# Attention: the norms' steps in a lasting PSUM tile, the values loaded last, and the causal mask of the maxima added by VectorE in the maximum's own instruction

## The chip, the cores and the metric

The kernel runs on one core of a Trainium2 chip. Its time is the device time of one execution, in microseconds (us). The engines of the core are called as in the profile: PE (TensorE's matmuls), PEld (its weight loads), DVE or VectorE, ACT or ScalarE, POOL or GpSimd, SP or SyncE, which here only issues DMAs. The kernel before was timed three times: 2924.38, 2925.44 and 2928.65 us, a median of 2925.44 us.

## The reference: what is computed

One decoder layer on 2048 tokens of width 1024. A norm and an input projection `z = h @ W_in` feed three mixers side by side: eight heads of attention with a forgetting gate, four heads of mLSTM, four of HGRN2. Their outputs are joined, projected back and added to `x`; a gated feed-forward layer with a short convolution follows. The change lies in the eight attention heads:

```python
qa = _rms(_heads(a_q, A_HEADS), a_q_g)
ka = _rms(_heads(a_k, A_HEADS), a_k_g)
ca = jnp.cumsum(jax.nn.log_sigmoid(a_f.astype(f32)), axis=1).transpose(0, 2, 1)
...
s = jnp.einsum('bhqd,bhkd->bhqk', qi, k) * scale
s = s + ci[..., None] - c[:, :, None, :]
s = jnp.where(kpos[None, :] <= qpos[:, None], s, -jnp.inf)
p = jax.nn.softmax(s, axis=-1)
return jnp.einsum('bhqk,bhkd->bhqd', p, v)
...
ya = _rms(_merge(oa), g_a.reshape(A_HEADS, HEAD_DIM)).reshape(bsz, t, A_DIM)
```

So each head has scores with a causal mask, a softmax, a product with the values, and then a norm over the 64 columns of each token of the head's output.

## The kernel before, in words

The program runs through four stages: the input projection with the mLSTM and HGRN2 mixers woven in, the attention, the output projection with the second norm (`phase_out`), and the feed-forward layer. Inputs and results of a stage go through DRAM tiles (`s_qh`, `s_ql`, `s_kh`, `s_kl` for queries and keys, each number split in a high and a low part, `s_v` for values, `s_y` for the mixers' output).

**The attention** is written out by hand in one order (`manual_schedule`): what an engine does is queued in the order in which the code issues it. The unit is a step: 128 keys against a block of 512 queries. A head has 4 blocks of queries with 4, 8, 12 and 16 steps, so 40 steps, and eight heads have 320. In a step of the loop (lines 1041 to 1063)

- `att_scores` makes the transposed scores of the step, keys on partitions, on PE (lines 912 to 917), `exp` and a rounded copy on ACT (919, 921), and leaves the low part `pl` of the result to a subtraction (925). In three steps of four POOL does this at once, in the fourth VectorE does it one step later;
- `att_maxima` goes on with the maxima, which run up to 22 steps ahead (`LEAD`; 12 are made before the first step): PE makes one block of plain scores `m`, 128 queries by up to 512 keys (872). Where the block touches the diagonal, a second matmul adds the triangle mask `mnat` through an identity (876). VectorE takes the maximum of each row (877). When the maxima of 512 queries are there, they are joined (883), turned by PE into a row (889) and written into the rows 64 to 67 of `QB` by VectorE (890), so that the scores' matmul subtracts them;
- `att_values` multiplies the values with the results of three steps earlier (`SKEW`), three matmuls (938 to 940), the last of which needs `pl`.

One block is 40, 128 or 16 such steps later turned into the output: when the last values of a block are in, ACT copies them out one step later (946), and two steps after that PE turns them (952) into the PSUM tile `x`, out of which VectorE copies (955). `Later` is the list of such work that is put off by a number of steps.

**The norm of a head** (`att_finish`) starts four steps after its last values: reciprocals of the sums (978), squares on ACT (981), their totals (984), then `scale` (987, 988), and four `link`s, one a step, which run the iteration for the reciprocal root (`rms_steps`, lines 120 to 132: three operations before the loop, and three rounds of three). All tiles of it lie in SBUF, 128 partitions by 16 elements. Then `times` (997, 998) multiplies the output, POOL the gain (1003), and SP stores to `s_y` (1008). `scale` comes 9 steps after the head's last values. The last head does this per block, with 4 elements instead of 16.

**PSUM** has eight banks, all in use here: three for `m`, two for the scores, two for the values' products and one for the tile `x`, which holds the turned maxima (4 by 128) and the turned outputs (128 by 260) by turns.

**The loads of a head** (`att_load`) are issued on SP's queue, in this order: `QB`, `KB` (what the maxima need, and half of the scores), the first four blocks of the values `V`, `QA`, `KA` (the scores' other half), and the rest of `V`. An issue waits on SP until the buffer is free and its source has been written, and what is queued behind it waits too. Heads 0 and 1 are loaded ahead of the first maxima, head h+1 at the third step of head h.

**Before the attention** `consts` brings the masks in through a scratch tile `craw`; `state` clears the state `cstate` of HGRN2.

Of the kernel before, what the change touches and what calls it, by code (L numbers as in the profile page):

```python
# [10 lines left out]
F32 = mybir.dt.float32  # L11
# [218 lines left out]
def z_stats(k, pz, xbufs):  # L230

    nc = k.nc
    ss = k.t(pz, [P, 8], tag="n8s", bufs=1)
# [598 lines left out]
def att_load(k, h, st):  # L832
# [13 lines left out]
    ld(KB[68:70], k.s_fc[h])  # L846
    v = k.s_v[:, h, :].rearrange("(jt p) c -> p jt c", p=P)
    ld(V[:, 0:4], v[:, 0:4])
    ld(QA[0:64], k.s_qh[r])
    ld(QA[64:128], k.s_ql[r])  # L850
    ld(KA[0:64], k.s_kl[r])
    ld(KA[64:128], k.s_kh[r])
    ld(V[:, 4:16], v[:, 4:16])


def att_maxima(k, sts, pa, ps, later):

    nc = k.nc
    for st in sts:
        for qb in range(4):  # L860
# [4 lines left out]
            for i in range(4):  # L865
                q0 = qb * BLK + i * P
                for kb in range(qb + 1):
# [4 lines left out]
                    nc.tensor.matmul(  # L872
                        m[:, 0:nn], QB[0:70, q0 : q0 + P], KB[0:70, kb * BLK : kb * BLK + nn], start=True, stop=not last
                    )
                    if last:
                        nc.tensor.matmul(m[:, n - P : n], k.identb, k.mnat, start=False, stop=True)
                    nc.vector.tensor_reduce(mx[:, i, kb : kb + 1], m[:, 0:n], axis=AX.X, op=ALU.max)  # L877
                    if i < 3 or not last:
# [51 lines left out]
def att_values(k, st, pa, ps, later, qb, j, c0, ph, pl):  # L930
# [27 lines left out]
    if h == AH - 1:  # L958
        att_finish(k, st, pa, 4 * qb, 4, later, 4)
    elif qb == 3:  # L960
        att_finish(k, st, pa, 0, 16, later, 4)


def att_finish(k, st, pa, t0, n, later, wait):

# [3 lines left out]
    bufs = 1 if n == 16 else 2  # L969
    pieces = [slice(i, i + 4) for i in range(0, n, 4)]  # L970

    def first():
        o = st["o"][:, t0 : t0 + n, :]
        w["num"] = o[:, :, 0:64]
# [3 lines left out]
        nc.vector.reciprocal(w["rl"], o[:, :, 64])  # L978

# [6 lines left out]
    def scale():  # L986
        nc.vector.tensor_tensor(w["ss"], w["ss"], w["rl"], op=ALU.mult)
        nc.vector.tensor_tensor(w["ss"], w["ss"], w["rl"], op=ALU.mult)
        w["s"] = k.t(pa, [P, n], tag=f"as{n}", bufs=bufs)
        w["chain"] = rms_steps(k, pa, w["s"], w["ss"], HD, 1.0, f"a{n}")  # L990

# [17 lines left out]

    i = wait  # L1010
# [17 lines left out]
def attention(k, pa, ps, side):  # L1028
# [528 lines left out]
def _trunk(ctx, tc, a, out):  # L1557
# [37 lines left out]
    with ExitStack() as ms:  # L1595
# [13 lines left out]
        with ExitStack() as zs:  # L1609
# [111 lines left out]
def state(k, mconst):  # L1721
# [14 lines left out]
    k.cstate = mconst("cstate", [P, 2, HD])  # L1736
    nc.vector.memset(k.cstate, 0.0)


def consts(k, a, cp, mconst, pz, psum, cm):  # L1740
# [3 lines left out]
    def cast(dst, src):  # L1744
        raw = cm.tile([P, P], F32, tag="craw", name=k.nm("craw"))[:, 0 : src.shape[1]]
# [4 lines left out]
    k.mnat = mconst("mnat", [P, P], BF16)  # L1750
# [99 lines left out]
```

## Time and profile before

| What | Number |
|---|---|
| the three timed runs, median | 2925.44 us |
| the profiled execution, its own time | 2926.52 us |
| its span in the trace | 2924.7 us |
| mean granted PE clock over the span | 0.979 |
| busy share of the span: PE, PEld, DVE, ACT, POOL | 96, 80, 68, 44, 49 % |
| the attention in the trace: first maximum's matmul, last values' matmul | 932.0 us, 1427.8 us |

The profile is of one execution, 1.8 us of which lie around the span and 1.1 us over the median. A row of a group gives the line, engine, operation and tiles, then the busy time, the mean of one, and the idle time of the engine ahead of them with what ended most of it. A row of a timeline gives the start, the duration, the engine, line and operation, and in brackets the idle time ahead of it and what ended it; PE's matmuls overlap, so the distance between two starts says more than a duration. A row of stretches gives the stretch, then its length and for each engine its busy time and number of instructions, then PE's granted clock (1.00 is full speed), the DMA engines' busy share and GB/s.

### The profile page before, as it was taken

Reading aid. Unit: us, or ns where it says so; the run is one execution under the profiler, and the core shown is the slowest. Engines: PE = TensorE matmul, PEld = TensorE weight load, DVE = VectorE, ACT = ScalarE, POOL = GpSimd, SP = SyncE. Lnnn points to the kernel's source line nnn. Section 1 sums busy time; section 2 is a strip of 40 time slices with the busy share of each in tenths; the row PEclk is TensorE's granted clock in tenths of the full one; section 3 lists DMA queues with packets and bytes.
Section 4 is the critical chain, followed back from the end, with each engine's and each line's share of the span. In section 5 each row is a group of like instructions: output and inputs, shape, how many; then the busy total and the mean of one; then the engine's idle time right before and its main releaser. Section 6 shows DMA issues by size and latency. Waiting matters only on the chain. (4 is left out here: it accounts for less than half of the span.)

```text
span 2924.7 us, 42911 instructions
## 1 busy us (share of the span) xinstructions
PE 2815.1 (96%) x15181; PEld 2344.7 (80%) x15181; DVE 1991.4 (68%) x3384; ACT 1280.3 (44%) x2167; POOL 1447.5 (49%) x1255
## 2 busy tenths in 40 slices
PE   8999998999999999999899899999999999999999
PEld 7899996989997666666688788888788788888887
DVE  7336787265777787778546676777787577777655
ACT  4223322131322878887423344444454343344443
POOL 2345462344354677776302466666475544444443
PEclk9999997999998999999999999999999999999999
DMA  5434444323225644451347444444778333333666
GB/s 161 126 96 144 136 127 133 102 95 116 89 89 154 119 97 89 87 109 27 108 166 233 146 161 159 160 150 157 258 249 270 110 103 108 108 105 120 233 211 210
DMA packets 346616, 411.08 MB, mean 141 GB/s; under 512 B 47650, under 2 KB 234096, under 8 KB 343232
## 3 DMA queue, kind: packets, MB, share of 16 engines
q1 hardware_dynamic: 292016, 318.45, 37.1%
q10 hardware_dynamic: 51952, 81.45, 7.6%
q0 software_dynamic: 2432, 8.42, 0.8%
q8 instruction: 120, 1.97, 0.3%
q14 instruction: 96, 0.79, 0.1%
HBM read 280.24 MB, written 127.98 MB: 140 GB/s over the span
## 5 line engine op out<-in xcount | busy, mean ns | idle before, releaser
L1248 POOL TENSOR_TENSOR w<-w,w 128x512 fp32r<-128x512 f32 x302 | 405.1, 1355 | 402.3 <-ACT w L1247 355.3
L1436 PE MATMUL ps<-w,w 128*128 128x512 f32 x1848 | 423.8, 391 | 3.6 <-ACT w L1427 1.9
L1436 PEld LDWEIGHTS ps<-w,w 128*128 128x128 f32 x1848 | 348.4, 189 | 78.2 <-ACT w L1427 2.4
L214 PE MATMUL w<-whi,hlo 128*128 128x256 f32 (+1 forms) x1280 | 374.3, 293 | 0.0
L214 PE MATMUL w<-whi,hhi 128*128 128x256 f32 (+1 forms) x1280 | 372.1, 291 | 2.0 <-DVE z L330 2.0
L214 PE MATMUL w<-wlo,hhi 128*128 128x256 f32 (+1 forms) x1280 | 372.7, 292 | 0.0
L925 POOL TENSOR_TENSOR pl<-pf,ph 128x512 fp32r<-128x512 f32 (+2 forms) x240 | 287.3, 1211 | 141.3 <-ACT ph L921 127.9
L1429 POOL TENSOR_TENSOR w<-w,w 128x512 fp32r<-128x512 f32 x154 | 215.6, 1407 | 204.5 <-ACT w L1427 165.8
L1247 ACT ACTIVATE w<-w 128x512 fp32r<-128x512 f32 x302 | 180.5, 627 | 263.5 <-POOL w L1248 86.0
L1428 DVE TENSOR_TENSOR w<-w,w 128x512 fp32r<-128x512 f32 x154 | 178.2, 1166 | 108.3 <-ACT w L1426 103.2
L214 PEld LDWEIGHTS w<-whi,hhi 128*128 128x128 f32 x1280 | 248.6, 194 | 3.7 <-DVE z L330 2.4
L214 PEld LDWEIGHTS w<-wlo,hhi 128*128 128x128 f32 x1280 | 248.5, 194 | 1.6 <-issue 0.2
L214 PEld LDWEIGHTS w<-whi,hlo 128*128 128x128 f32 x1280 | 248.4, 194 | 1.3 <-issue 0.2
L877 DVE TENSOR_REDUCE mx<-m 128x1 f32<-128x512 f32 (+2 forms) x320 | 190.7, 605 | 85.4 <-PE m L872 59.1
L195 POOL TENSOR_TENSOR wlo<-wraw,whi 128x512 fp32r<-128x512 f32 (+1 forms) x112 | 147.9, 1352 | 147.0 <-ACT whi L193 124.5
L1253 DVE TENSOR_TENSOR w<-w,w 128x512 f32<-128x512 f32 x176 | 151.5, 879 | 86.6 <-DMA w<-in_w_up_dram 76.8
L919 ACT ACTIVATE pf<-s 128x512 f32<-128x512 f32 (+1 forms) x320 | 172.4, 539 | 85.1 <-PE s L913 49.4
L921 ACT ACTIVATE ph<-pf 128x512 fp32r<-128x512 f32 (+1 forms) x320 | 185.1, 578 | 12.9 <-DMA s_v<-h 2.7
L1294 DVE SCALAR_TENSOR_TENSOR u<-ps,fcol,u 128x1023 f32<-128x1023 f32 x88 | 108.9, 1278 | 95.0 <-ACT u L1293 95.0
L940 PE MATMUL pv<-pl,V 128*65 128x512 f32 (+1 forms) x320 | 120.3, 376 | 25.9 <-DVE pl L925 25.1
L1427 ACT ACTIVATE w<-w 128x512 fp32r<-128x512 f32 x154 | 96.7, 628 | 110.9 <-PE ps L1436 88.5
L1426 ACT ACTIVATE w<-w 128x512 fp32r<-128x512 f32 x154 | 95.8, 622 | 93.0 <-POOL w L1429 45.6
(374 smaller groups left out, 7062.3 us busy)
## 6 DMA issues: line engine op xcount, KB each, us to landing
w<-in_w_up_dram SPq DMA_DIRECT2D x182, 256.0 KB
w<-s_g SPq DMA_DIRECT2D x154, 256.0 KB
w<-in_w_down_dram SPq DMA_DIRECT2D x110, 256.0 KB
wraw<-in_w_in_dram SPq DMA_DIRECT2D x48, 512.0 KB
s_g<-u ACTq DMA_DIRECT2D x88, 256.0 KB
w<-s_w SPq DMA_DIRECT2D x88, 256.0 KB
s_g<-w ACTq DMA_DIRECT2D x66, 256.0 KB
x<-in_x_dram SPq DMA_DIRECT2D x32, 512.0 KB
```

Source lines behind the costliest of these rows:

```text
L195: nc.gpsimd.tensor_tensor(lo[:, q + i : q + i + 2, :], raw[:, i : i + 2, :], h[:, i : i + 2, :].bitcast(F32), op=ALU.subtract)
L214: nc.tensor.matmul(out, lsl(lhs[a], i), rsl(rhs[b], i), start=(i == 0 and j == 0), stop=(i == n - 1 and j == 2))
L877: nc.vector.tensor_reduce(mx[:, i, kb : kb + 1], m[:, 0:n], axis=AX.X, op=ALU.max)
L919: nc.scalar.activation(pf[:, c0:], s[:, c0:], AF.Exp)
L921: nc.scalar.activation(ph[:, c0:], pf[:, c0:], AF.Copy)
L925: eng.tensor_tensor(pl[:, c0:], pf[:, c0:], ph[:, c0:].bitcast(F32), op=ALU.subtract)
L1247: nc.scalar.activation(h, t, AF.Copy)
L1248: nc.gpsimd.tensor_tensor(lo, t, h.bitcast(F32), op=ALU.subtract)
L1253: nc.vector.tensor_tensor(t, x, y, op=op)
L1428: nc.vector.tensor_tensor(gl, gr, gh.bitcast(F32), op=ALU.subtract)
L1429: nc.gpsimd.tensor_tensor(wl, wr, wh.bitcast(F32), op=ALU.subtract)
L1436: nc.tensor.matmul(tiles[tile], g[x][:, tile * P : (tile + 1) * P], w[y], start=j == 0 and c == 0, stop=j == nj - 1 and c == 2,)
```

## The change

Five edits in the attention, and what makes room for them.

1. `att_maxima`: the mask's matmul is gone. Where the block touches the diagonal, VectorE's maximum becomes one instruction that adds the mask (`mnat`, now 512 wide with zeros in front) to the block in PSUM, writes the sum back there, and gives the maximum. The built program has it as two rows, the instruction and one that writes its result out.
2. The turned maxima (`put`) take a buffer of `m`'s three instead of the tile `x`.
3. The bank of `x` is now one tile that lasts through the attention, `k.px`: 260 columns for the turned outputs, and three slices of 48 columns in which `scale` and the `link`s of a norm keep their sums and results (`rms_psum`). `scale` computes the reciprocals a second time, into PSUM. The very last block still works in SBUF.
4. `scale` of a whole head comes 15 steps after its last values instead of 9.
5. `att_load` issues both pieces of `V` last. Of head 0, the second piece is issued after the first twelve maxima; head 1 is loaded in the seventh step instead of ahead of everything.

Room in SBUF comes from `craw`, whose part `cstate` takes (it is cleared after the masks are in), and from joining some small tiles.

```diff
@@ att_load
     ld(KB[68:70], k.s_fc[h])
-    v = k.s_v[:, h, :].rearrange("(jt p) c -> p jt c", p=P)
-    ld(V[:, 0:4], v[:, 0:4])
     ld(QA[0:64], k.s_qh[r])
...
     ld(KA[64:128], k.s_kh[r])
+    yield
+    v = k.s_v[:, h, :].rearrange("(jt p) c -> p jt c", p=P)
+    ld(V[:, 0:4], v[:, 0:4])
+    yield
     ld(V[:, 4:16], v[:, 4:16])
@@ att_maxima
-                        m[:, 0:nn], QB[0:70, q0 : q0 + P], KB[0:70, kb * BLK : kb * BLK + nn], start=True, stop=not last
+                        m[:, 0:nn], QB[0:70, q0 : q0 + P], KB[0:70, kb * BLK : kb * BLK + nn], start=True, stop=True
                     )
                     if last:
-                        nc.tensor.matmul(m[:, n - P : n], k.identb, k.mnat, start=False, stop=True)
-                    nc.vector.tensor_reduce(mx[:, i, kb : kb + 1], m[:, 0:n], axis=AX.X, op=ALU.max)
+                        nc.vector.tensor_tensor_reduce(
+                            out=m[:, 0:n],
+                            in0=m[:, 0:n],
+                            in1=k.mnat[:, BLK - n :],
+                            scale=1.0,
+                            scalar=NEG,
+                            op0=ALU.add,
+                            op1=ALU.max,
+                            accum_out=mx[:, i, kb : kb + 1],
+                        )
+                    else:
+                        nc.vector.tensor_reduce(mx[:, i, kb : kb + 1], m[:, 0:n], axis=AX.X, op=ALU.max)
...
-                pm = k.t(ps["x"], [4, P], tag="x")
+                pm = k.t(ps["m"], [P, BLK], tag="m")[0:4, 0:P]
@@ turn
-        pt = k.t(ps["x"], [P, 4, 65], tag="x")
+        pt = k.px[:, 0:260].rearrange("p (a d) -> p a d", a=4)
@@ rms_psum, new; att_finish
+    for _ in range(3):
+        yield
+        nc.vector.tensor_tensor(u, out, h, op=ALU.mult)
+        nc.vector.tensor_tensor(u, u, out, op=ALU.mult)
+        nc.vector.scalar_tensor_tensor(out, u, 1.5, out, op0=ALU.add, op1=ALU.mult)
...
+        k.pn = (k.pn + 1) % 3
+        pn = k.px[:, 260 + 48 * k.pn : 308 + 48 * k.pn].rearrange("p (a n) -> p a n", a=3)
+        ps, ms, w["s"] = (pn[:, i, 0:n] for i in range(3))
+        nc.vector.reciprocal(ms, w["sum"])
+        nc.vector.tensor_tensor(ss, ss, ms, op=ALU.mult)
+        nc.vector.tensor_tensor(ps, ss, ms, op=ALU.mult)
+        w["chain"] = rms_psum(k, pa, w["s"], ps, ms, f"a{n}")
...
-    i += 1
+    i = 15 if n == 16 else i + 1
     later.put(i, scale)
@@ attention
-        att_load(k, 0, sts[0])
-        att_load(k, 1, sts[1])
+        first = att_load(k, 0, sts[0])
+        next(first)
+        next(first)
+
+        k.px, k.pn = k.t(ps["x"], [P, BLK], tag="x"), 0
...
-                        if h and qb == 0 and j == SKEW - 1 and h + 1 < AH:
-
-                            att_load(k, h + 1, sts[h + 1])
+                        if (qb, j) == ((0, SKEW - 1) if h else (1, 2)) and h + 1 < AH:
+
+                            for _ in att_load(k, h + 1, sts[h + 1]):
+                                pass
```

**How the instructions move, on SP**, where the attention begins. Each row is the load of one piece for head 0 and, in brackets, the semaphores it waits for; `PE`, `Activation` and `Pool` there mean that a buffer must come free. Before:

```order
L840 DMA KB_9751<-s_fc 2x2048 [waits DMAHW3_49]
L840 DMA V_9752<-s_v 128x4x130 [waits PE_49,DMAHW4_49,Activation_49,Pool_49]
L840 DMA QA_9748<-s_qh 64x2048 [waits DMAHW5_49]
L840 DMA QA_9748<-s_ql 64x2048 [waits DMAHW6_49]
L840 DMA KA_9749<-s_kl 64x2048 [waits DMAHW7_49]
L840 DMA KA_9749<-s_kh 64x2048 [waits DMAHW0_49]
L840 DMA V_9752<-s_v 128x12x130 [waits DMASW6_49,DMASW7_49,DMASW4_49,DMAHW1_49,DMASW2_49,DMASW0_49]
```

and of the change:

```order
L840 DMA KB_9738<-s_fc 2x2048 [waits DMAHW3_49]
L840 DMA QA_9735<-s_qh 64x2048 [waits DMAHW4_49]
L840 DMA QA_9735<-s_ql 64x2048 [waits DMAHW5_49]
L840 DMA KA_9736<-s_kl 64x2048 [waits DMAHW6_49]
L840 DMA KA_9736<-s_kh 64x2048 [waits DMAHW7_49]
L840 DMA V_9739<-s_v 128x4x130 [waits PE_49,DMAHW0_49,Activation_49,Pool_49]
L840 DMA V_9739<-s_v 128x12x130 [waits DMASW6_49,DMASW7_49,DMASW4_49,DMAHW1_49,DMASW2_49,DMASW0_49]
```

The four loads of `QA` and `KA` are no longer behind the piece of `V` that waits for PE, ACT and POOL.

**On VectorE**, where the norm of head 0 begins while head 1 is worked on (`ass` holds the totals, `rl` the reciprocals, `mx` the maxima, `ao` the turned outputs, `pl` the low parts). Before, from `scale` on:

```order
L987 TENSOR_TENSOR ass_1694_10701<-ass_1694_10701,rl_1692_10699 128x16 [waits DVE_49]
L988 TENSOR_TENSOR ass_1694_10701<-ass_1694_10701,rl_1692_10699 128x16 [waits DVE_49]
L120 TENSOR_SCALAR a16m_10806<-ass_1694_10701 128x16 [waits DVE_49]
L121 TENSOR_SCALAR a16h_10807<-ass_1694_10701 128x16
L122 TENSOR_SCALAR as_1725_10805<-a16m_10806 128x16 [waits DVE_49]
L877 TENSOR_REDUCE mx_10601<-m_10821 128x1 [waits PE_49]
```

and of the change, where `x_9750` is the lasting tile:

```order
L937 TENSOR_TENSOR pl_10809<-pf_10805,ph_10807 128x512 [waits Activation_49,Pool_49]
L878 ISA m_10844,mx_10558<-m_10844,mnat 128x512 [waits PE_49]
L878 ISA mx_10558 128x1
L895 TENSOR_REDUCE m_1744_10847<-mx_10558 128x4 [waits DVE_49]
L1030 RECIPROCAL x_9750<-ao_10012 128x16
L1031 TENSOR_TENSOR ass_1682_10656<-ass_1682_10656,x_9750 128x16 [waits DVE_49]
L1032 TENSOR_TENSOR x_9750<-ass_1682_10656,x_9750 128x16 [waits DVE_49]
L981 TENSOR_SCALAR x_9750<-x_9750 128x16 [waits DVE_49]
L982 TENSOR_SCALAR a16h_10855<-x_9750 128x16 [waits DVE_49]
L983 TENSOR_SCALAR x_9750<-x_9750 128x16 [waits DVE_49]
L967 COPY ao_10721<-x_9750 128x260 [waits DVE_49,PE_49]
```

`scale` has six operations instead of five and now stands right ahead of the copy of the second block's output of head 1, out of the same bank.

**On PE** at that same place, the end of the step in which the second block of head 1 is turned. Before:

```order
L872 MATMUL m_10914<-KB_9767,QB_9766 128x512 [waits DVE_49]
L876 LDWEIGHTS identb
L876 MATMUL m_10914<-mnat,identb 128x128
L938 MATMUL pv_10879<-ph_10855,V_9768 65x512
L939 MATMUL pv_10879<-ph_10855,V_9768 64x512
L940 MATMUL pv_10879<-pl_10857,V_9768 65x512 [waits Pool_49]
L952 MATMUL x_10925<-ident,oT_10885 128x65 [waits Activation_49]
```

and of the change:

```order
L874 MATMUL m_10844<-KB_9933,QB_9932 128x512 [waits DVE_49]
L950 MATMUL pv_10813<-ph_10792,V_9934 65x512
L951 MATMUL pv_10813<-ph_10792,V_9934 64x512
L952 MATMUL pv_10813<-pl_10794,V_9934 65x512 [waits Pool_49]
L964 MATMUL x_9750<-ident,oT_10817 128x65 [waits DVE_49,Activation_49]
```

The mask is gone, and the transposes wait for VectorE as well as for ACT: in the built program for the last operation of `scale`, L983. This wait stands at the second block of each of the heads 1 to 7, so seven times, and nowhere else among the turns.

More of the change, by code (lines that the diff above doesn't have):

```diff
@@ L232, in z_stats @@
     nc = k.nc
-    ss = k.t(pz, [P, 8], tag="n8s", bufs=1)
+    ss = k.t(pz, [P, 16], tag="ss")[:, 0:8]
     for b in range(2):
@@ L958, in att_values, with rms_psum, att_finish @@
     if h == AH - 1:
-        att_finish(k, st, pa, 4 * qb, 4, later, 4)
+        att_finish(k, st, pa, 4 * qb, 4, later)
     elif qb == 3:
-        att_finish(k, st, pa, 0, 16, later, 4)
-def att_finish(k, st, pa, t0, n, later, wait):
+        att_finish(k, st, pa, 0, 16, later)
+def rms_psum(k, pool, out, ss, ms, tag):
+    nc = k.nc
+    h = k.t(pool, list(ss.shape), tag=tag + "h")
+    u = k.t(pool, list(ss.shape), tag=tag + "u")
+    nc.vector.tensor_scalar(out=ms, in0=ss, scalar1=1.0 / HD, scalar2=EPS, op0=ALU.mult, op1=ALU.add)
+    nc.vector.tensor_scalar(out=h, in0=ss, scalar1=-0.5 / HD, scalar2=-0.5 * EPS, op0=ALU.mult, op1=ALU.add)
+    nc.vector.tensor_scalar(
+        out=out.bitcast(I32), in0=ms.bitcast(I32), scalar1=-0.5, scalar2=float(0x5F3759DF), op0=ALU.mult, op1=ALU.add
+    )
+    for _ in range(3):
[3 more added lines that the diff above has]
+        nc.vector.scalar_tensor_tensor(out, u, 1.5, out, op0=ALU.add, op1=ALU.mult)
+    yield
+def att_finish(k, st, pa, t0, n, later):
     nc = k.nc
@@ L970, in att_finish @@
     pieces = [slice(i, i + 4) for i in range(0, n, 4)]
+    end = st["h"] == AH - 1 and t0 == 12
     def first():
         o = st["o"][:, t0 : t0 + n, :]
-        w["num"] = o[:, :, 0:64]
+        w["num"], w["sum"] = o[:, :, 0:64], o[:, :, 64]
         w["rl"] = k.t(pa, [P, n], tag=f"rl{n}", bufs=bufs)
@@ L977, in first @@
         w["ss"] = k.t(pa, [P, n], tag=f"ass{n}", bufs=bufs)
-        nc.vector.reciprocal(w["rl"], o[:, :, 64])
+        nc.vector.reciprocal(w["rl"], w["sum"])
     def square(c):
@@ L986, in scale @@
     def scale():
[L987 to L990, printed above, removed]
+        ss, rl = w["ss"], w["rl"]
+        if end:
+            nc.vector.tensor_tensor(ss, ss, rl, op=ALU.mult)
+            nc.vector.tensor_tensor(ss, ss, rl, op=ALU.mult)
+            w["s"] = k.t(pa, [P, n], tag=f"as{n}", bufs=bufs)
+            w["chain"] = rms_steps(k, pa, w["s"], ss, HD, 1.0, f"a{n}")
+            return
+        k.pn = (k.pn + 1) % 3
[5 more added lines that the diff above has]
+        w["chain"] = rms_psum(k, pa, w["s"], ps, ms, f"a{n}")
     def link():
@@ L1008, in store @@
         nc.sync.dma_start(k.s_y[t0 * P : (t0 + n) * P, r].rearrange("(tt p) d -> p tt d", p=P), w["sq"])
-    i = wait
+    i = 4
     later.put(i, first)
@@ L1039, in attention @@
             later.step()
+        for _ in first:
+            pass
         lead, pend, t = LEAD0, [], 0
@@ L1618, in _trunk @@
             z = z_groups(k, 0, pz, wp, psw, xb)
-            pz.tile([P, 120], F32, tag="padz", name="padz", bufs=1)
+            pz.tile([P, 128], F32, tag="padz", name="padz", bufs=1)
             state(k, mconst)
@@ L1749, in consts @@
     k.identb = mconst("identb", [P, P], BF16)
-    k.mnat = mconst("mnat", [P, P], BF16)
+    k.mnat = mconst("mnat", [P, BLK], BF16)
+    nc.vector.memset(k.mnat[:, 0 : BLK - P], 0.0)
     k.mtr = mconst("mtr", [P, P], BF16)
@@ L1754, in consts @@
     nc.vector.tensor_copy(k.identb, k.ident)
-    cast(k.mnat, a["mnat"])
+    cast(k.mnat[:, BLK - P :], a["mnat"])
     cast(k.mtr, a["mtr"])
@@ L1759, in consts @@
         cast(k.cmask[:, i, :], a["cmask"][:, i * HD : (i + 1) * HD])
+    nc.vector.memset(k.cstate, 0.0)
     k.sel8 = mconst("sel8", [72, BH])
@@ L1793, in consts @@
     lg = k.col[:, 24:26]
-    lm, lr, lb = mconst("lm", [P, 2]), mconst("lr", [P, 2]), mconst("lb", [P, 2])
+    lbs = mconst("lbs", [P, 6, 2])
+    lm, lr, lb, k.lba, k.lbb, k.lbn = (lbs[:, i, :] for i in range(6))
     nc.vector.tensor_tensor(lm, lg, lg, op=ALU.subtract)
```

5 lines of the change are left out of this document (2 added, 3 removed).

## The prediction

> **What bounds the kernel now.** I read the profile from the top: busy shares, then the stretches of the attention, then what PE waits for there, then the timelines of PE and VectorE around one of those waits. The page's first part:
>
> ```profile
> PE 2815.1 (96%) x15181; PEld 2344.7 (80%) x15181; DVE 1991.4 (68%) x3384; ACT 1280.3 (44%) x2167; POOL 1447.5 (49%) x1255
> ```
>
> PE is busy for 96% of the span, so time is won only by taking matmuls away or by closing PE's gaps. The stretches (length; busy us and count of PE, PEld, DVE, ACT, POOL; PE's clock; DMA share; GB/s) show where gaps are: the attention's start, its middle, and around one stall in the middle.
>
> ```profile
> 932.00:960.00 28.00, 24.14 (x88) 15.27 (x87) 19.90 (x41) 10.71 (x22) 13.82 (x21) 0.63 0.91 229
> 960.00:1378.00 418.00, 400.81 (x2116) 274.81 (x2115) 327.18 (x623) 338.86 (x644) 295.56 (x253) 0.98 0.44 87
> 1024.00:1029.00 5.00, 5.00 (x27) 3.18 (x26) 4.86 (x10) 4.30 (x9) 3.43 (x3) 1.00 0.83 223
> 1029.00:1032.00 3.00, 0.66 (x4) 0.16 (x3) 3.00 (x5) 1.20 (x2) 2.86 (x3) 1.00 0.00 0
> 1032.00:1035.60 3.60, 3.60 (x12) 2.19 (x12) 3.23 (x8) 1.23 (x2) 2.87 (x4) 0.57 0.01 2
> ```
>
> In the middle PE idles 418.00 - 400.81 = 17.2 us. The last three rows are one event: VectorE full for 5 us, then PE nearly idle for 3 us while VectorE is still full, then 3.6 us at clock 0.57. The second half of the event costs 3.60 x (1 - 0.57) = 1.55 us. What PE waits for in the whole attention (total, times, longest), and the waits themselves (idle time ahead in brackets):
>
> ```profile
> PE pv L940 <- DVE pl L925: 25.1, 17, 3.0
> ```
>
> ```profile
> 1031.89 0.45 PE L940 MATMUL pv<-pl,V 128*65 128x512 f32 x1 [2.34 <-DVE pl L925]
> 1341.27 0.33 PE L940 MATMUL pv<-pl,V 128*65 128x256 f32 x1 [0.23 <-DVE pl L925]
> 1382.46 0.33 PE L940 MATMUL pv<-pl,V 128*65 128x256 f32 x1 [3.04 <-DVE pl L925]
> 1392.34 0.44 PE L940 MATMUL pv<-pl,V 128*65 128x512 f32 x1 [2.50 <-DVE pl L925]
> 1399.45 0.44 PE L940 MATMUL pv<-pl,V 128*65 128x512 f32 x1 [1.51 <-DVE pl L925]
> 1404.49 0.33 PE L940 MATMUL pv<-pl,V 128*65 128x256 f32 x1 [0.99 <-DVE pl L925]
> ```
>
> Of the 17 waits, seven are long ones, one in each of the heads 1 to 7 (first and last: 1031.89 and 1382.46); seven are short like that at 1341.27; the last three rows are the last head's. So the long ones hold 25.1 - 5.0 - 7 x 0.24 = 18.4 us, 2.6 each. Why VectorE is late there:
>
> ```profile
> 1020.17 0.17 DVE L987 TENSOR_TENSOR ass<-ass,rl 128x16 f32<-128x16 f32 x1
> 1020.96 0.69 DVE L877 TENSOR_REDUCE mx<-m 128x1 f32<-128x512 f32 x1
> 1021.77 0.18 DVE L131 TENSOR_TENSOR a16u<-a16u,a16h 128x16 f32<-128x16 f32 x1
> 1023.70 1.22 DVE L131 TENSOR_TENSOR a16u<-a16u,a16h 128x16 f32<-128x16 f32 x1
> 1024.96 1.22 DVE L132 SCALAR_TENSOR_TENSOR as<-a16u,as 128x16 f32<-128x16 f32 x1
> 1030.09 1.75 DVE L925 TENSOR_TENSOR pl<-pf,ph 128x512 fp32r<-128x512 f32 x1
> 1033.87 0.41 DVE L955 COPY ao<-x 128x260 f32<-128x260 f32 x1
> ```
>
> ```profile
> L877 DVE TENSOR_REDUCE mx<-m 128x1 f32<-128x512 f32 (+2 forms) x320 | 190.7, 605 | 85.4 <-PE m L872 59.1 <-PE m L876 23.2
> ```
>
> The same 128x16 operation of a `link` takes 0.18 us at 1021.77 and 1.22 at 1023.70. Both have all their operands in SBUF. The 320 maxima, which read PSUM, keep to a mean of 605 ns. So the links sometimes wait for SBUF, the queue behind them slips, and `pl` comes 2.3 to 3.0 us late.
>
> **The change part by part**, against the profiled execution's own 2926.52 us (1.1 over the median).
>
> *The masks leave PE.* 128 matmuls of this kind go:
>
> ```profile
> L876 PE MATMUL m<-mnat,identb 128*128 128x128 bf16 x128 | 31.0, 242 | 0.0
> ```
>
> ```profile
> 1021.95 0.23 PE L876 MATMUL m<-mnat,identb 128*128 128x128 bf16 x1
> 1021.99 0.31 PE L938 MATMUL pv<-ph,V 128*65 128x256 f32 x1
> 1022.14 0.28 PE L939 MATMUL pv<-ph,V 128*64 128x256 f32 x1
> 1022.25 0.28 PE L940 MATMUL pv<-pl,V 128*65 128x256 f32 x1
> ```
>
> Since matmuls overlap, the 242 ns are an upper end (31 us in all). From start to start a mask takes 0.04 us, the lower end (5 us), and the matmul behind it 0.15 instead of the 0.11 of the next one. I take 0.07: **-9 us**.
>
> *VectorE gets the masks.* No masked maximum is in this trace. The nearest rows are a plain maximum (0.69 at 512 columns, above), an operation of VectorE on two inputs that writes into PSUM, and one with all operands in SBUF:
>
> ```profile
> L1330 DVE TENSOR_TENSOR ps<-ps,tmp 128x512 f32<-128x512 f32 x44 | 30.5, 693 | 0.4
> L1428 DVE TENSOR_TENSOR w<-w,w 128x512 fp32r<-128x512 f32 x154 | 178.2, 1166 | 108.3 <-ACT w L1426 103.2 <-issue 3.5 <-DMA s_g<-u 1.4
> ```
>
> The price lies between no more than now and 1.17 - 0.69 = 0.48 more each; I take the 693 ns, since it is the row with PSUM, and for the read-out that follows up to 0.17, as a 128x16 operation has. That is 128 x 0.17 = 22 us of VectorE's time, and 62 + 22 = 84 at the upper end. VectorE has 418.00 - 327.18 = 91 us of slack in the middle, so this hides unless it stands ahead of something that PE awaits (the last rival). The maxima run up to 22 steps ahead; that is the cover.
>
> *The norm's steps in PSUM.* They take no SBUF result any more but for `h` and `u`. If they stay at the 0.17 to 0.18 us of the undisturbed rows, as PSUM's maxima keep theirs, the 2.1 us that two operations lost at 1023.70 and 1024.96 are not lost, and `scale` and the links, which ran at 1020 to 1027, come six steps later, behind the `pl` that was late. Then the seven long waits and the last head's three go: 18.4 + 5.0 = **-23.4 us**; I leave the seven short ones. With the long ones goes the half clock behind them: 7 x 1.55 = **-10.9 us**. (After the last head's 2.50, 1.51 and 0.99 I count no drop; one row shows it, below.) The lower bound is nothing gained: third rival.
>
> ```profile
> 1392.30:1396.00 3.70, 3.22 (x14) 1.90 (x15) 3.63 (x8) 1.18 (x3) 2.98 (x4) 1.00 0.14 38
> ```
>
> *A new wait.* The transposes of the second block in heads 1 to 7 now wait for the last operation of `scale`, which is issued in the same step. On PE all the next steps are queued behind them, ACT and POOL wait for those. The pace of a step, before:
>
> ```profile
> 1024.83 0.40 PE L912 MATMUL s<-QB,KB 70*128 70x512 f32 x1
> 1025.30 0.40 PE L872 MATMUL m<-KB,QB 70*128 70x512 f32 x1
> 1026.24 0.39 PE L912 MATMUL s<-QB,KB 70*128 70x512 f32 x1
> ```
>
> A step is 1.41 us, and its maxima's matmul is done 0.9 in. Then VectorE does, in this order, the masked maximum (0.7), its read-out (up to 0.2), the join (0.2) and six operations of `scale` (five took 1020.96 - 1020.17 = 0.79, so about 1.0). It ends 3.0 us in, or 3.6 if the `pl` ahead of the maximum holds it up for 0.6. The transposes are due at 1.41, so PE waits 1.6 to 2.2; I take 2.0: 7 x 2.0 = **+14 us**. Idle times of 2.34 were followed by half clock, 2.50 once was not and 1.51 was not, so I give four of seven the drop: 4 x 1.55 = **+6.2 us**. The links behind it stand in the steps 16 to 19, three short operations each, and have that much slack.
>
> [...] Without the wait the sum would be 20 us lower.
>
> *The turned maxima* take one of three buffers of `m` for the time from PE's transpose to VectorE's write; that is 32 times, hidden by the 22 steps of lead, and it costs a wait of at most one step each if VectorE is late. I count nothing.
>
> *The start.* SP's queue, PE and ACT there:
>
> ```profile
> 915.06 0.25 SPq L840 DMA_DIRECT2D KB<-s_fc  x1
> 929.22 0.39 SPq L840 DMA_DIRECT2D V<-s_v  x1
> 931.49 0.59 SPq L840 DMA_DIRECT2D KA<-s_kh  x1
> ```
>
> ```profile
> 942.35 0.79 PE L913 MATMUL s<-QA,KA 128*128 128x512 f32 x1 [1.33 <-DMA KA<-s_kh]
> ```
>
> ```profile
> 947.59 0.63 ACT L921 ACTIVATE ph<-pf 128x512 fp32r<-128x512 f32 x1 [2.69 <-DMA s_v<-h]
> ```
>
> `V` stood for 929.22 - 915.06 = 14 us at the queue's head, and `QA`, `KA` behind it. Now they go ahead of it, past a wait that is not theirs. PE's busy time in 932 to 960 is 24.1 of 28 at clock 0.63, so much of this is work. I take the two waits, 1.33 + 2.69: **-4 us**, between 0 and -7 (with part of the 28 x 0.37 = 10 us of clock). Eight masked maxima among the first twelve, with no lead yet, cost 8 x 0.17: **+1 us**. Head 1's loads, moved from the start to the seventh step, and the second piece of `V` have some ten steps (14 us) until they are needed, and the DMA share of 0.44 leaves room: nothing. If that cover is short, the first maxima of head 1 or the values of head 0 wait, once each.
>
> Sum: -9 - 23.4 - 10.9 + 14 + 6.2 - 4 + 1 = -26.1, so 2900.4 for a profiled execution, 2899.3 for a median that lies 1.1 lower; **2900 us**.
>
> **The rivals.** Without the new wait the sum stands at 2880.2.
>
> *The new wait is longer.* `pl` and the maximum both late, 3.3 us each time and a clock drop each time: 7 x (3.3 + 1.55) = 34, 2914. For: VectorE was full for 7.9 of the 8 us from 1024 to 1032, at that very place. Against: the links that filled it have moved away.
>
> *No clock drop at the new wait.* With 1 us each time 2887; with 2 us and no drop 2894. For: 1.51 and 2.50 without a drop. Against: 2.34 with one. [...]
>
> *The norm's steps gain nothing.* They stay slow with `h` and `u` in SBUF, the old waits stay and the new one is added: 2880.2 + 34.3 + 20.2 = 2935. Against: every PSUM row keeps its time.
>
> *Slower: VectorE takes the masks badly.* If a masked maximum with its read-out costs 0.5 or more over the plain one, three or four in a row ahead of `scale` leave VectorE as late at the turn as it is today, when the copy at 1033.87 comes 5.9 us behind the transposes:
>
> ```profile
> 1027.94 0.41 PE L952 MATMUL x<-ident,oT 65*128 65x65 f32 x4
> ```
>
> Then PE waits 5.9 there: 7 x (5.9 + 1.55) = 52, 2932. It decides for slower from (2926.5 - 2880.2) / 7 - 1.55 = 5.1 us of wait in each head. For: 1166 ns of the SBUF row. Against: 693 of the PSUM row.
>
> **How the numbers follow.** Forecast 0.52; longer wait 0.20; no drop 0.12; no gain from PSUM 0.07; masks slow 0.09. The range holds the first three: down to the 2887 with 7 us more from the masks or the start, 2880; up to the 2914 with the masks at 5 instead of 9 and no gain at the start, 2922. A measurement can tell about 0.2%, 5.9 us, from no change: faster means below 2919.6, slower above 2931.3. Faster: 0.84 of the three, less 0.04 for their upper edges, 0.80. Slower: the two rivals' 0.16 lie around 2932 to 2935 with both signs near, 0.10. The same: 0.10.
>
> **What would show it.** Right: in the waits of PE the one on `pl` falls from 25.1 to a few us, and a new one of the transposes on VectorE appears, seven times, 14 us; the stretch of half clock follows some of them; a masked maximum with its read-out takes 0.7 to 0.9 us at 512 columns; the norm's 128x16 rows take 0.17 to 0.2; the first score of `QA` waits for no `KA`. Wrong: the old waits stay, or the new one is over 3 us; masked rows above 1.1 us; a new wait of PE on `m`, because VectorE returns its buffers late; or a start that does not move.

## The result and the profile after

| | Median, us | Range, runs |
|---|---|---|
| before | 2927.05 | 2924.38 to 2928.74, 4 |
| the change | 2910.06 | 2908.00 to 2916.08, 4 |
| ratio | 0.9950 | 95% interval 0.9936 to 0.9963 |

The change saves 17 us of the 26 that were forecast; the time lies inside the range. A second set of runs gave 2910.96 against 2925.08, a ratio of 0.9960 (0.9947 to 0.9972). The profiled execution took 2909.49 us with a span of 2907.7.

What PE waits for in the attention of the changed kernel (total, times, longest):

```profile
PE x L964 <- DVE x L983: 13.9, 7, 3.4
PE m L874 <- DVE mx L878: 5.6, 2, 5.5
PE pv L952 <- DVE pl L937: 5.2, 10, 1.0
PE pv L952 <- POOL pl L937: 3.3, 5, 1.3
```

The old waits on `pl`, 25.1 us on VectorE and 0.7 on POOL before, have shrunk to 5.2 and 3.3. The first row is the new wait: seven times, 13.9 us, where the forecast had seven times 2.0. Five of the seven last 1.67 us, one 2.13, and the last one 3.42. The second row is one wait of 5.5 us at the start that the forecast did not have.

VectorE and PE at one of the seven turns, with the step's first matmul on PE at the top:

```profile
1019.80 0.39 PE L924 MATMUL s<-QB,KB 70*128 70x512 f32 x1
...
1023.04 0.44 PE L964 MATMUL x<-ident,oT 65*128 65x65 f32 x4 [1.67 <-DVE x L983]
```

```profile
1019.91 0.68 DVE L937 TENSOR_TENSOR pl<-pf,ph 128x512 fp32r<-128x512 f32 x1
1020.71 0.70 DVE L878 CUSTOM_DVE_ANT_0 m<-m,mnat 128x512 f32<-128x512 f32 x1
1021.32 0.14 DVE L878 DVE_READ_ACCUMULATOR2_ANT mx<- 128x1 f32 x1
1021.50 0.17 DVE L895 TENSOR_REDUCE m<-mx 128x4 f32<-128x16 f32 x1
1021.58 0.25 DVE L1030 RECIPROCAL x<-ao 128x16 f32<-128x16 f32 x1
...
1022.71 0.18 DVE L983 TENSOR_SCALAR x<-x 128x16 int32<-128x16 int32 x1
1023.51 0.43 DVE L967 COPY ao<-x 128x260 f32<-128x260 f32 x1 [0.62 <-PE x L964]
```

Masked maximum, read-out, join and the six operations of `scale` follow each other without a gap and end 3.1 us into the step. PE was ready for the transposes 1.67 us before they began, at 1021.37, so 1.57 us into the step (the forecast had 1.41). No operation of the rows shown is slow; PE waits because they stand in the same step and the built order has its transposes wait for the last of them. At the last of the seven turns (1370.43) a `pl` of 1.66 us stood ahead of them, and the wait is 3.42.

The groups on VectorE (count, then busy time and mean ns); the second row is the plain maximum:

```profile
L878 DVE CUSTOM_DVE_ANT_0 m<-m,mnat 128x512 f32<-128x512 f32 x32 | 22.2, 693 | 2.3 <-PE m L874 1.5
L889 DVE TENSOR_REDUCE mx<-m 128x1 f32<-128x512 f32 x192 | 130.7, 686 | 61.9 <-PE m L874 59.5
L878 DVE DVE_READ_ACCUMULATOR2_ANT mx<- 128x1 f32 x128 | 17.9, 140 | 0.0
L990 DVE SCALAR_TENSOR_TENSOR x<-a16u,x 128x16 f32<-128x16 f32 x21 | 3.7, 178 | 0.7
```

A masked maximum of 512 columns takes 693 ns, and its read-out 140 ns. The links' last operation has a mean of 178 ns, where it had 522 before:

```profile
L132 DVE SCALAR_TENSOR_TENSOR as<-a16u,as 128x16 f32<-128x16 f32 x21 | 11.0, 522 | 0.7
```

The clock behind four of the seven waits, two with and two without a drop (length, then for each engine busy time and count, then the clock, DMA share, GB/s):

```profile
1024.30:1027.70 3.40, 3.40 (x10) 2.39 (x9) 1.47 (x10) 2.25 (x4) 1.27 (x1) 0.50 0.02 5
1082.30:1089.10 6.80, 6.80 (x21) 4.80 (x22) 2.06 (x12) 2.76 (x5) 1.64 (x2) 0.50 0.00 0
1258.00:1262.00 4.00, 4.00 (x21) 2.66 (x20) 2.74 (x16) 3.55 (x7) 1.56 (x2) 1.00 0.02 4
1313.00:1318.00 5.00, 5.00 (x26) 3.35 (x25) 3.55 (x18) 4.08 (x7) 1.82 (x2) 1.00 0.02 5
```

All four followed a wait of 1.67 us at a turn, the first of them the one at 1023.04 above:

```profile
1082.26 0.65 PE L964 MATMUL x<-ident,oT 65*128 65x65 f32 x4 [1.67 <-DVE x L983]
1256.66 0.44 PE L964 MATMUL x<-ident,oT 65*128 65x65 f32 x4 [1.67 <-DVE x L983]
1312.41 0.44 PE L964 MATMUL x<-ident,oT 65*128 65x65 f32 x4 [1.67 <-DVE x L983]
```

The clock fell behind four of the seven, as forecast, but twice for 6.8 us instead of 3.4 (at 1082.30 and, within the wait of 3.42, at 1369.02).

To leave out what the stages before and after the attention do, I compare one distance in every trace, from the scores' matmul of the fifth step to the last matmul of the values, and call it the middle. Before, after, and after in a second trace:

```profile
951.73 0.63 PE L912 MATMUL s<-QB,KB 70*128 70x512 f32 x1
...
1427.79 0.28 PE L940 MATMUL pv<-pl,V 128*65 128x256 f32 x1
```

```profile
947.02 0.63 PE L924 MATMUL s<-QB,KB 70*128 70x512 f32 x1
...
1408.56 0.28 PE L952 MATMUL pv<-pl,V 128*65 128x256 f32 x1
```

```profile
951.22 0.63 PE L924 MATMUL s<-QB,KB 70*128 70x512 f32 x1
...
1412.56 0.28 PE L952 MATMUL pv<-pl,V 128*65 128x256 f32 x1
```

The middle takes 476.1 us before and 461.5 and 461.3 after: **14.6 us** of gain, the same in both traces. The first trace also came to the fifth step 4.7 us earlier, the second only 0.5 earlier. What stands ahead of the attention differs only in a few small tiles (where they lie and when they are cleared), and in the traces of the kernels below the fifth step starts anywhere from 946.6 to 953.1, so I do not put these 4 us down to the change.

### The profile page after: what moved, and what is told of

It reads as the page before. It is cut to its first block, busy times and chain, and to the rows that moved or that the text cites. A ratio compares the mean times of both kernels' runs of the same rounds, so it can differ in the third digit from the quotient of the medians.

```text
span 2907.7 us, 42807 instructions
## 1 busy us (share of the span) xinstructions
PE 2799.3 (96%) x15053; PEld 2343.7 (81%) x15053; DVE 1961.4 (67%) x3523; ACT 1278.8 (44%) x2167; POOL 1446.1 (50%) x1255
## 5 line engine op out<-in xcount | busy, mean ns | idle before, releaser
L889 DVE TENSOR_REDUCE mx<-m 128x1 f32<-128x512 f32 x192 | 130.7, 686 | 61.9 <-PE m L874 59.5
L874 PE MATMUL m<-KB,QB 70*128 70x512 f32 (+2 forms) x320 | 130.6, 418 | 5.6 <-DVE mx L878 5.6
```

## The experiments

Each row is the median of its own runs, the ratio to before with its interval, and from its trace the middle and the waits of PE in it.

| Kernel | Median, us | Ratio (95%) | Middle, us | Turn waits on VectorE, us | Waits on `pl`, us |
|---|---|---|---|---|---|
| before (four sets) | 2924.90 to 2929.86 | 1 | 476.1 | 0 | 25.8 |
| the change (PSUM, step 15) | 2910.06 | 0.9950 (0.9936 to 0.9963) | 461.5 | 13.9 | 8.5 |
| scale at 16 | 2889.73 | 0.9871 (0.9853 to 0.9889) | 440.4 | 0 | 9.7 |
| scale at 18 | 2904.16 | 0.9936 (0.9924 to 0.9948) | 452.6 | 0 | 18.7 |
| PSUM, step 9 | 2920.73 | 0.9987 (0.9978 to 0.9995) | 471.2 | 19.5 | 7.3 |
| PSUM, step 9, product in SBUF | 2900.18 | 0.9919 (0.9905 to 0.9932) | 453.8 | 3.4 | 10.7 |
| SBUF, step 9, whole heads | 2914.32 | 0.9969 (0.9957 to 0.9980) | 467.7 | 4.1 | 22.0 |
| SBUF, step 15, whole heads | 2924.59 | 1.0000 (0.9990 to 1.0011) | 473.4 | 0 | 16.4, and 9 more on maxima |
| mask on PE, step 15 | 2915.70 | 0.9958 (0.9943 to 0.9973) | 464.1 | 13.3 | 7.0 |
| mask on PE, step 16 | 2904.40 | 0.9928 (0.9909 to 0.9947) | 444.4 | 0 | 7.8 |
| loads of before | 2912.06 | 0.9941 (0.9924 to 0.9958) | 458.8 | 13.9 | 8.6 |

**Is the new wait what eats the gain?** One number is changed:

```diff
-    i = 15 if n == 16 else i + 1
+    i = 16 if n == 16 else i + 1
```

> The changed kernel with scale and the links one step later (16 instead of 15), so that they stand behind the turn of the second block. Theory A (the 13.9 us in seven waits of the transposes on VectorE, and the half clock behind four of them, are lost only to the place of scale): these waits vanish, the half clock with them, nothing takes their place; 2910 - 14 - 8 = 2888, between 2884 and 2894. Theory B (VectorE is late at that place anyway, and the wait only moves to the next matmul that needs pl): a wait of PE on pl of some 2 us per head appears at the next step; 2904 to 2912.

What PE waits for in the attention of this kernel:

```profile
PE pv L952 <- DVE pl L937: 8.3, 9, 2.0
PE m L874 <- DVE mx L878: 5.3, 2, 5.1
```

No turn waits on VectorE any more, and one half-clock stretch of 3.4 us is left in the middle instead of four. The median falls to 2889.73. Theory A gave 2888. Waits of 0.95 us on `pl` appear once in each of six heads, half of what theory B asked for, without a drop. So the place of `scale` alone costs the change some 20 us: 13.9 of waiting, and 17 us at half clock, which is 8.5 (an estimate: time at half clock is counted half).

The changed kernel again, for its trace:

> The changed kernel as it is, once more, beside the kernels of this call and for its trace. Both theories: 2908 to 2916; seven waits of the transposes on VectorE with 13 to 14 us in all. If the 5 us by which the stage ahead of the attention was shorter in the first trace are chance, they are gone or smaller here while the waits in the attention stay; if the change brings them, they are here again.

It gave 2910.96 us and seven waits of 13.8 us in all; the head start was gone (above).

**Is it the bank or the step?** The norm's steps in PSUM at the old steps 9 to 12:

```diff
-    i = 15 if n == 16 else i + 1
+    i += 1
```

> The changed kernel with scale and the links in PSUM, but at the old steps 9 to 12, where no turn stands in the same step. Theory A (PSUM alone keeps the norm's operations short; the step only must not be that of a turn): 128x16 rows of 0.17 to 0.25 us, no wait at the turn, no long wait on pl, 2886 to 2896, like the version at step 16. Theory B (at these steps VectorE is full from the maxima and the totals anyway): waits of PE on pl of 1 to 2 us in each head, some with half clock, 2897 to 2908.

Both theories missed. The waits on `pl` went as A said, but the turn waits more than in the change, and for another operation, the multiplication of `times`:

```profile
PE x L964 <- DVE asq L1041: 19.5, 7, 4.4
PE pv L952 <- DVE pl L937: 6.6, 15, 1.6
```

```profile
1025.77 1.69 DVE L937 TENSOR_TENSOR pl<-pf,ph 128x512 fp32r<-128x512 f32 x1
1027.38 0.69 DVE L878 CUSTOM_DVE_ANT_0 m<-m,mnat 128x512 f32<-128x512 f32 x1
1027.99 0.14 DVE L878 DVE_READ_ACCUMULATOR2_ANT mx<- 128x1 f32 x1
1028.16 0.17 DVE L895 TENSOR_REDUCE m<-mx 128x4 f32<-128x16 f32 x1
1028.25 0.41 DVE L1041 TENSOR_TENSOR asq<-ao,x 128x256 f32<-128x256 f32 x1
```

With `scale` at 9 the four multiplications stand in steps 13 to 16, and the third reads its factor out of the lasting bank in step 15. It is queued behind a `pl` that took 1.69 and a masked maximum. My premise that no use of the bank stood in a turn's step was wrong: I had counted `scale` and the links only. The mended theory, that PE waits for whatever VectorE still has to do in that bank, was then tried by moving only that reading:

```diff
         if c.start == 0:
-            nc.vector.tensor_tensor(w["s"], w["s"], w["rl"], op=ALU.mult)
+            s = k.t(pa, [P, n], tag=f"as{n}", bufs=bufs)
+            nc.vector.tensor_tensor(s, w["s"], w["rl"], op=ALU.mult)
+            w["s"] = s
```

> The norm's steps in PSUM at steps 9 to 12 with one edit: the first operation of times writes its product into a tile in SBUF, and the four multiplications of step 13 to 16 read that, so that none of them touches the lasting bank in the turn's step 15. Theory A (what PE waits for at the turn is whatever operation VectorE has in that bank in the same step, in the run before the 19.5 us for a multiplication of times): the wait goes, 2888 to 2898. Theory B (steps 9 to 16 are too full on VectorE): waits on pl take its place, 2905 to 2920.

The turn waits fall from 19.5 to 3.4, all of it once in the last head, where the first multiplication still reads the bank, and the time by 20 us to 2900.18. So the mechanism of theory A holds, while the time lies 2 us above its range and below that of theory B:

```profile
PE pv L952 <- DVE pl L937: 9.5, 21, 1.6
PE m L874 <- DVE mx L878: 4.7, 5, 0.9
PE x L964 <- DVE as L1041: 3.4, 1, 3.4
```

It is slower than step 16 by some 10 us, with more short waits on `pl` and on the maxima. A later place does not help either:

```diff
-    i = 15 if n == 16 else i + 1
+    i = 18 if n == 16 else i + 1
```

> The changed kernel with scale at step 18: every operation in the lasting bank, from scale at 18 to the last multiplication at 25, stands between the turns of steps 15 and 27. Theory A: as at step 16, no wait at the turn, 2886 to 2894; the 0.95 us that pl is late once a head there may go as well. Theory B (step 16 was a lucky place): a wait on VectorE of 1 us or more per head, 2898 or more.

No turn waits, as A said, but `pl` is late twice in most heads, 0.8 to 1.6 us each in the middle heads and 18.7 us in all, and the time is 2904.16: this is theory B, a wait on VectorE in each head. Of the free places tried, 16 is the best, and not because of the bank alone.

**Does PSUM bring anything?** All norms in SBUF, by the branch that the last block takes, first at step 15 and then, with `i += 1` as above, at step 9:

```diff
-    end = st["h"] == AH - 1 and t0 == 12
+    end = True
```

> The changed kernel with all norm steps in SBUF as before (one reciprocal), but still from step 15 on; the lasting tile holds only the turned outputs, so that the transposes wait for no norm step. Theory A (PSUM is what keeps the links at 0.17 us; in SBUF some of them take 1.2 us beside other SBUF work): slow 128x16 rows return, waits of PE on pl of 2 to 3 us in most heads with half clock behind them; 2908 to 2920. Theory B (the later step alone removed the old waits): no slow rows, no waits at the turn; 2886 to 2893.

> The changed kernel with the norm's steps in SBUF and at the old steps 9 to 12: of the change only the masks on VectorE, the lasting tile for the turned outputs and the loads stay. Theory A (the gain of the old waits comes from PSUM alone): the long waits on pl of before are back, 20 to 25 us with half clock behind six or seven, less 8 us of masks: 2914 to 2924. Theory B (masks on VectorE make it worse in SBUF, as the 2946 at step 15 may say): 2930 or more.

They took 2946.39 and 2932.15 us, ratios of 1.0058 (1.0040 to 1.0077) and 1.0025 (1.0013 to 1.0036). The first lies far above both theories, the second in theory B's range. But these numbers hold something else. At the end of the attention of the second,

```profile
PE ty L1162 <- DMA yin<-s_y: 11.8, 1, 11.8
```

and 12.0 in the first: with more tiles in SBUF the built program issued the first load of the next stage behind all of the last head's stores. The test was spoilt at its end, so I ran both again with SBUF steps for whole heads only, in tiles that left that order as it is in the change (the edit for step 15; for step 9 it has `i += 1` besides):

```diff
+        if n == 16:
+            nc.vector.tensor_tensor(ss, ss, rl, op=ALU.mult)
+            nc.vector.tensor_tensor(ss, ss, rl, op=ALU.mult)
+            w["s"] = k.t(pa, [P, n], tag=f"as{n}", bufs=bufs)
+            w["chain"] = rms_psum(k, pa, w["s"], ss, w["sq"][:, n - 1, 0:n], f"a{n}")
+            return
         k.pn = (k.pn + 1) % 3
```

> As the kernel with the norm's steps in SBUF from step 15 on, again only for the norms of whole heads, with the end of the changed kernel. Theory A (a 128x16 operation in SBUF stands for 1.2 us when POOL works at the same time, wherever it is put): slow rows at step 15 to 18, waits of PE on pl and on the maxima, 2918 to 2930. Theory B (the later step is free of the trouble, and the 2946 was the end alone): 2895 to 2905.

> As the kernel with the norm's steps in SBUF at steps 9 to 12, but only for the norms of whole heads; the last head's norms stay as in the changed kernel, so that the end of the attention has the order of the changed kernel again (in the earlier run PE waited 11.8 us there for a load behind the stores). Theory A (SBUF costs 25 us of waits on pl as before, and the rest of the 2932 was the end): 2912 to 2922, 6 or 7 long waits on pl. Theory B (SBUF together with masks on VectorE is dearer in the middle too): 2926 or more.

At step 15 theory A holds: 2924.59, no gain at all over before. VectorE and POOL at the place where `scale` runs:

```profile
1022.42 0.66 DVE L1028 TENSOR_TENSOR ass<-ass,rl 128x16 f32<-128x16 f32 x1
1023.11 1.22 DVE L1029 TENSOR_TENSOR ass<-ass,rl 128x16 f32<-128x16 f32 x1
1024.36 0.17 DVE L981 TENSOR_SCALAR asq<-ass 128x16 f32<-128x16 f32 x1
1024.44 1.29 DVE L982 TENSOR_SCALAR a16h<-ass 128x16 f32<-128x16 f32 x1
...
1026.53 0.17 DVE L988 TENSOR_TENSOR a16u<-as,a16h 128x16 f32<-128x16 f32 x1
```

```profile
1021.75 3.95 POOL L937 TENSOR_TENSOR pl<-pf,ph 128x512 fp32r<-128x512 f32 x3 [1.37 <-ACT ph L933]
```

From 1021.75 to 1025.70 POOL makes three `pl` without a pause, 1.3 us each, and VectorE's 16-column operations take up to 1.2 and 1.3 us; the two long ones end at 1024.33 and 1025.73, where the second and third `pl` do (about 1024.38, by thirds of the 3.95 us, and 1025.70). At 1026.53, with POOL idle, 0.17. In the change POOL was as busy beside the norm's operations of 1021.58 to 1022.89, which took 0.17 to 0.25 there (above):

```profile
1020.92 2.50 POOL L937 TENSOR_TENSOR pl<-pf,ph 128x512 fp32r<-128x512 f32 x2 [1.37 <-ACT ph L933]
```

Of the two long rows, that at 1023.11 (1.22) has both operands in SBUF, that at 1024.44 (1.29) its only one; the same two operations took 0.18 and 0.17 in the change, with an operand in PSUM (1022.07 and 1022.50). The rows show that the long ones end with POOL's `pl`; what holds them, no run here shows. At step 9 theory A holds as well (2914.32): the SBUF version gains 10.6 us by its median, 8 from the masks (below) and little else, with 21.3 us of waits on `pl` by VectorE left. So the old waits go only with PSUM: at the same steps 9 to 12 they are 6.6 us with the norm in PSUM.

**What is a mask worth?** The mask's matmul back on PE and a plain maximum on VectorE, at step 15 and at step 16:

```diff
-                    if last:
-                        nc.vector.tensor_tensor_reduce(...)
-                    else:
-                        nc.vector.tensor_reduce(mx[:, i, kb : kb + 1], m[:, 0:n], axis=AX.X, op=ALU.max)
+                    if last:
+                        nc.tensor.matmul(m[:, n - P : n], k.identb, k.mnat[:, BLK - P :], start=False, stop=True)
+                    nc.vector.tensor_reduce(mx[:, i, kb : kb + 1], m[:, 0:n], axis=AX.X, op=ALU.max)
```

> The changed kernel with the causal mask of the maxima added on PE by a matmul as before; VectorE takes a plain maximum. Theory A (each mask costs PE 0.07 us, and VectorE's read-out and masked maximum cost PE only 0.2 us at each of the seven turns): 128 x 0.07 - 7 x 0.2 = +7.5, 2915 to 2920. Theory B (the masks on PE lay beside other work of PE): within 2 us of 2910. Theory C (VectorE's masked maxima are what makes the turn late): the wait at the turn falls below 1 us, and the time to 2900 or less.

> The version with scale at step 16, with the causal mask of the maxima added on PE by a matmul. There are no waits at the turn here that could hide what a mask costs. Theory A (0.065 us of PE for each of 128 masks): 8 us more than the version at step 16, so 2896 to 2900 where that has 2888 to 2892. Theory B (they fill gaps of PE): within 2 us of it.

The medians are 2915.70 at step 15 (A's range) and 2904.40 at step 16, where A said 2896 to 2900. The runs of the latter lie between 2890.24 and 2907.99: two under 2893 at a mean granted clock of 0.983, four over 2903 at 0.979 to 0.980. Such a spread hides 8 us, so I go by the middles of the traces, one for each kernel, and take out what the clock and the waits did. At step 15 the middle is 2.5 us longer with masks on PE, though PE waits 2.1 less (20.3 against 22.4) and stands at half clock for 13.7 us instead of 20.5, which is worth 3.4. So the masks cost 2.5 + 2.1 + 3.4 = 8.0. At step 16: 4.0 longer, 1.9 less waiting, 1.7 less for the clock, 7.6. That is 0.06 to 0.07 us for each of some 120 masks that lie in the middle. Theory C falls: the wait at the turn is 13.3 instead of 13.9, so the masked maxima are not what makes VectorE late there.

**The start.** All loads as before (V's first piece ahead of `QA` and `KA`, heads 0 and 1 ahead of everything):

```diff
     ld(KB[68:70], k.s_fc[h])
+    v = k.s_v[:, h, :].rearrange("(jt p) c -> p jt c", p=P)
+    ld(V[:, 0:4], v[:, 0:4])
     ld(QA[0:64], k.s_qh[r])
...
-        first = att_load(k, 0, sts[0])
-        next(first)
-        next(first)
+        att_load(k, 0, sts[0])
+        att_load(k, 1, sts[1])
```

> The changed kernel with the loads of before (V's first piece ahead of QA and KA, heads 0 and 1 loaded ahead of everything). Theory A (the early loads of QA and KA delay the stores of the projection's last pieces, ACT and VectorE behind them, and so the second maxima's matmul by 5.5 us, which takes away what the scores win): the wait of m on VectorE falls to about 1 us, a wait of 1 us on KA and a later first values' matmul return, the time moves by less than 3 us: 2907 to 2913. Theory B (the step of the prediction, loads gain 4 us): 2913 to 2917.

The median is 2912.06, in theory A's range, though only 1 us from theory B's, so the rows have to decide, and they are theory A's: PE's wait of 5.5 us has fallen to 1.7, and waits of 1.6 on `KA` and 1.8 on ACT are back. One store of `s_v` and the ACT operation that needs its buffer, in the change:

```profile
921.75 0.57 POOL L345 DMA_DIRECT2D s_v<-h  x1 [0.30 <-POOL h L342]
```

```profile
930.28 0.42 ACT L341 ACTIVATE h<-z 128x256 fp32r<-128x256 f32 x1 [10.36 <-DMA s_v<-h]
```

and with the loads of before:

```profile
921.46 0.57 POOL L345 DMA_DIRECT2D s_v<-h  x1 [0.30 <-POOL h L342]
```

```profile
924.08 0.42 ACT L341 ACTIVATE h<-z 128x256 fp32r<-128x256 f32 x1 [4.45 <-DMA s_v<-h]
```

The same store holds ACT 8.5 us in the one and 2.6 in the other. In the change 2 MB of `QA` and `KA` are on their way then (issued from 910.10 on, with the loads of before from 924.72 on). The DMA engines around that store, the change first (share and GB/s are the last two numbers):

```profile
920.00:925.00 5.00, 3.82 (x32) 3.62 (x31) 1.48 (x2) 0.00 (x0) 4.68 (x4) 1.00 1.03 223
```

```profile
920.00:925.00 5.00, 4.13 (x35) 3.93 (x33) 1.19 (x2) 0.42 (x1) 4.68 (x4) 1.00 0.14 55
```

So in the change what ACT and VectorE still have to do for the projection comes late, with the maxima behind it. With the loads of before the collision comes later instead: there ACT waits 10.77 us for a store of `s_qh`, until 938.65, where the change has a wait of 4.02 until 935.87. From the first maximum's matmul to the fifth step both orders take about the same: 947.02 - 927.17 = 19.9 us in the change, 947.08 - 926.91 = 20.2 with the loads of before, and 19.7 in the kernel before. The middle is 2.7 us shorter with the loads of before (458.8 against 461.5) at the same waits, but this is the clock: four drops of 3.4 us instead of 20.5 us at half clock, worth 3.4.

## Why the prediction was right, and where it was off

The direction and the range held, and the likeliest case with its mechanism is what happened, at a little over half of its size in the traces' middle. By its steps:

| Step | Forecast, us | Measured, us |
|---|---|---|
| masks leave PE | -9 | -8.0 and -7.6 |
| old waits on `pl` | -23.4 | -17.3 (25.1 + 0.7 to 5.2 + 3.3) |
| clock, old and new waits together | -10.9 + 6.2 = -4.7 | -1.7 |
| the new wait at the turn | +14 | +13.9 |
| the start | -4 + 1 | 0 |
| sum | -26.1 | -13.1 |

The traces' middle gained 14.6, the medians 17.0 and 14.1. Of the 13 us between the two sums, 6 are the old waits, 3 the clock, 3 the start and 1 the masks; all four were put too high.

- *The new wait* was sized by laying out one step by hand from rows of before (3.0 to 3.6 us into the step; measured 3.1). Six of the seven waits lie in the 1.6 to 2.2 that this gave; the seventh, 3.42, is the rival with `pl` and the maximum both late, once instead of seven times, and that the sum came so near 14 is partly luck. One wait was thus over the 3 us that the prediction named as a sign of being wrong. And the experiment at step 16 shows that the new wait was a true loss: with it the change is worth 0.5%, without it 1.3%.
- *The old waits.* "Then the seven long waits and the last head's three go" was too much. The seven went; of the last head's 5.0 us, 3 stay (0.63 and 1.01 on VectorE, 1.33 on POOL). The short ones, which the prediction left as they were, grew from 1.7 to 3.6 us on VectorE, and four on POOL, 2.0 us, come new in the middle heads.
- *The clock.* "Four of seven" came out, but by luck. The prediction went by the length of a wait; yet of the five waits of 1.67 us three were followed by a drop and two not, and that of 2.13 was not (the last section has what decides). That each drop costs 1.55 us was too low: the stretch 1032.00:1035.60 ends before its drop does, a drop of 3.4 us costs 1.7, and two of the new ones lasted 6.8. Before, seven drops of 3.4 us made 23.9 us at half clock, after, four made 20.5.
- *The start.* The step that failed: "past a wait that is not theirs". The loads did go past it. But that wait had also kept 2 MB off the DMA queues while the projection's last stores were landing (one of them held ACT for 2.6 us with the loads of before, 8.5 in the change). I priced the loads' own wait and not what they would collide with. Two of the signs of being wrong that the prediction lists are this step: a start that does not move, and a new wait of PE on `m` behind VectorE, 5.5 us.
- *VectorE's price of a mask* was put at the 693 ns of a PSUM row; measured 693, with a read-out of 140 (the upper end that the prediction did not take, 128 x 0.48, is 61 and not 62). The rival of slow masks is refuted by these rows, that of norm steps which gain nothing by the 0.17 us rows and by the SBUF versions.

Open: where the remaining 1.5 us between the sum and the middle lie; why step 18 leaves more waits on `pl` than 16, and step 9 more short ones, which was seen and not taken apart; and what SBUF would give at step 16, which was not run (at step 15 it has no turn waits and still gains nothing).

## What to carry to other kernels

Before you put small results into a spare part of a PSUM bank, list every operation that touches the bank, readers at the very end too, and the step in which the other engine needs it; here one step decided 21 of 36 us by which the middle can be shortened. Look at small operations of VectorE beside long ones of GpSimd: with all operands in SBUF some took 1.2 to 1.3 us here and ended where GpSimd's `pl` did, and with an operand in PSUM the same ones took 0.17 to 0.18. A load that is moved ahead of a wait also moves ahead of what that wait had protected: look at which stores are landing then (here one that held ACT for 8.5 us instead of 2.6). And compare two kernels by their waits and their time at half clock, not by the time alone: the same waits cost here up to 3.4 us more or less by the clock.

## What was not expected of the hardware

- The wait that drops the clock can be short, and need not drop it. 1.67 us of idle time were followed by 3.4 us at 0.50 (1024.30, and again 1198.35), by 6.8 us (1082.30), and twice by none (1258.00, 1313.00). What decided here is where the wait falls. In the middle of this trace the drops begin at 1024.27, 1082.30, 1198.35 and 1369.02, which are 17, 51 and 101 times 3.413 us after the first, and each lasts one or two such stretches. Laid on that grid, the wait ahead of 1082.30 falls into one stretch, and the two without a drop are split over two. The stretch that holds most of the wait, for each of these three (PE's busy time is the first number behind the length):

```profile
1078.89:1082.30 3.41, 1.74 (x9) 0.94 (x8) 2.91 (x11) 2.28 (x5) 2.13 (x2) 1.00 0.13 44
1252.97:1256.38 3.41, 2.02 (x9) 1.11 (x7) 3.09 (x11) 2.58 (x5) 2.06 (x3) 1.00 0.11 42
1310.99:1314.40 3.41, 1.99 (x12) 1.64 (x13) 2.29 (x14) 1.29 (x3) 1.83 (x2) 1.00 0.02 5
```

PE is busy for 1.74, 2.02 and 1.99 of 3.41 us, so it idles for 1.67, 1.39 and 1.42. In the middles of all fourteen traces here, no such stretch at full clock with up to 1.52 us of idle time was followed by half clock, all 42 with 1.73 or more were, and 18 of the 23 between. (The ends of PE's matmuls are modelled in the profile, so the border is no sharper than that.)

- The masked maximum's own instruction takes hardly longer than the plain one: 693 ns against 686 in the same trace for 512 columns, although it reads two inputs and writes 512 results. What it adds is the read-out row, 140 ns: from the start of one to the operation behind the read-out are 0.79 us (1020.71 to 1021.50).
